# Down products of two feed-forward layers as seven block products, with weight sums made by DMA copies

## The chip, the cores and the metric

The kernel runs on one core of a Trainium2 chip. The metric is the device time of one execution in microseconds (us). The core has a matrix engine (TensorE, PE in the profile, with its weight loads as PEld), VectorE (DVE), ScalarE (ACT), GpSimd (POOL) and SyncE (SP), which run their own instruction queues and meet at semaphores. Sixteen DMA engines move data for transfers that SP, ACT and GpSimd issue.

## The reference

Three blocks work on one sequence of 1024 positions with 1024 features, all in float32. Each has a mixing part (gated linear attention and a short convolution; two kinds of attention and a long convolution; spatial gating and pooling) and a feed-forward part. The change touches the second product of the first and of the third feed-forward part:

```python
# first block
h = h + jnp.square(jax.nn.relu(hn @ w_up[layer])) @ w_down[layer]
out = rms_norm(h, norm_final_w)
# third block
f = jnp.square(jax.nn.relu(h @ w_fc1)) @ w_fc2
x = x + gate2 * rms_norm_3(f, norm2_post)
```

`w_up` is 1024x4096, `w_down` is 4096x1024; `w_fc1` and `w_fc2` have the same sizes. The second block has a gated feed-forward part of its own.

## The kernel before

Activations lie with features on the 128 partitions and positions along the free axis. Every large product is made of three matmuls (`mm3`, L428): an operand is split into a rounded part hi (ACT copies it, L319) and the rest lo (DVE subtracts, L305), and hi-hi, hi-lo and lo-hi are added in PSUM. A matmul has a 128x128 stationary tile and up to 512 moving columns.

The feed-forward parts are called f1, f2 and f3. Their up products (`up7`, L895) are already made of seven block products over the halves of features and positions. Its loop goes over groups g (16 in f1 and f3, 22 in f2), each with 84 matmuls. The results get a square of a relu (`relu2`, L907) and go to a DRAM scratch `gd` by DMAs of ACT's queue (L910); the products of half the features for the first groups are parked in `sd` and read back through GpSimd's queue (`start`, L957). DVE writes into slots that are parts of `X1`.

The down products (`down7`, L1029) go through `CHUNKS`: 2 or 4 contraction tiles at a time. For a chunk the values are loaded from `gd`, split into `Hh` and `Hl`, the weights are loaded and split into ring slots, and eight output tiles times two halves of positions follow, each with one PSUM bank, which DVE adds to `X` (ACT copies in the first chunk). In the last chunk the sums of squares for the next norm are made as well: `sq_add` (L525) squares on ACT and adds on GpSimd, or on DVE for the second sum that f1 and f2 need. For f1 and f2 the residual is added to `X` by four accumulating DMAs of GpSimd (L1066). f3 takes its last chunk in parts of 512, 256 and 256 columns (`quarters`), and its tail (`tail`, L2267) normalises, adds the residual and stores.

All weights and all values of a down product come through one `Stream` (L148). It knows the units in order; `load` (L178) issues a unit's DMA on SP into a raw buffer, `_split` (L203) splits it into a ring slot, and two units are loaded ahead. Ring A has four slots, ring B two more in a down stage. Up and down stages have four raw buffers, until `drop_raws` (L786) leaves two. "ada" units, weights of a conditioning vector, are spread over f1 and f2: DVE multiplies and adds them in eight instructions each (`ada_unit`, L634).

The order of work is written out by hand: the program keeps a count `pe` of matmul time and steps background generators (`fine`, `step`) and the stream (`tick`, L246) between groups of matmuls. Each engine takes its instructions in order.

Of the kernel before, what the change touches and what calls it, by code (L numbers as in the profile page):

```python
# [57 lines left out]

def _feat(a):

    return np.ascontiguousarray(a.T.reshape(KT, P, a.shape[0]).transpose(1, 0, 2))


def lay_out(i):
# [17 lines left out]
    a["w1_down"] = i["w_down"][0].reshape(32, P, D)  # L82
# [24 lines left out]
    a["w3_down"] = i["w_fc2_3"].reshape(32, P, D)  # L107
# [40 lines left out]
class Stream:  # L148
# [5 lines left out]
    def __init__(self, k):  # L154
# [6 lines left out]
        self.raws = []  # L161
        self.groom = [False, False]
# [40 lines left out]
    def _split(self):  # L203
# [62 lines left out]


class Kern:
    def __init__(self, tc, a, out):
# [7 lines left out]
        self.adap = None  # L277

# [373 lines left out]
    CHUNKS = {"f1": [2, 2] + [4] * 7, "f2": [2] + [4] * 5, "f3": [2, 2] + [4] * 7}  # L652
# [5 lines left out]
    def setup(self):  # L658
# [46 lines left out]
        def ffn7(n, up, down, with_ada=0):  # L705
# [19 lines left out]
            S[n + "h"], S[n + "d"] = [], []  # L725
            gd = S[n + "x"] = self.drp.tile([a[down].shape[0], P, T], F32, name="gd" + n)
# [168 lines left out]
    def up7(self, name):  # L895
# [11 lines left out]
        def relu2(dst, src, m, t, scale=1.0):  # L907
            self.act(dst, src, AF.Relu, scale=scale)
            self.act(dst, dst, AF.Square)
            nc.scalar.dma_start(out=gd[m, :, 512 * t:512 * t + 512], in_=dst)  # L910
# [12 lines left out]
        for g in range(0, M, 2):  # L923
# [7 lines left out]
            for i in (0, 1):  # L931
# [7 lines left out]
                else:  # L939
                    relu2(s, ps[i], 2 * (g + i), 0)  # L940
# [7 lines left out]
        def slot():  # L948
            n[0] += 1
            return X1[:, (n[0] - 1) % 8]  # L950
# [6 lines left out]
        def start(g):  # L957

            ca = wide() if gated else None
            s1 = None  # L960
            if g < M:
                s1 = scratch() if gated else slot()
                nc.gpsimd.dma_start(out=s1, in_=sd[g])
                if gated:
                    nc.gpsimd.dma_start(out=ca[:, :512], in_=cd[g])
            return s1, ca

        nxt = start(0)
        for g, G in enumerate(groups):
# [18 lines left out]
            if g >= M:  # L988
# [4 lines left out]
                else:  # L993
                    relu2(slot(), z, 2 * g, 0)
# [11 lines left out]
            if not gated:  # L1006
                relu2(c22, c22, 2 * g + 1, 1)
# [4 lines left out]
            else:  # L1012
                relu2(c21, c21, 2 * g + 1, 0)
# [9 lines left out]
            else:  # L1023
                relu2(v, v, 2 * g, 1)
        W.groom[1] = True
        self.ext_es.close()
        self.open_ss()

# [123 lines left out]
    def block1(self):  # L1152
# [9 lines left out]
        lvl = gp.tile([P, 7, P], U8, name="lvl")  # L1162
        g0, g0_es = self.pool("gate0", 1, None, "right")
# [177 lines left out]
        self.open_ring("f1d", ada=True)  # L1341
        g = self.cols("norm_final_w")
        self.tt(self.g12, g, self.cols("ln1_g_2"), ALU.mult)
        a1, a2 = [], []
        self.down7("f1", self.add_ffn(a1, a2, g),
# [167 lines left out]
    def block2(self):  # L1513
# [243 lines left out]

        self.up7("f2")
# [268 lines left out]
    def block3(self):  # L2027
# [204 lines left out]
        self.hp, e = self.pool("hp2", 1, None, "right")  # L2232
        self.ffn_es.insert(0, e)
        ac = []

        def add(m, part, ps, first, last):
# [88 lines left out]
```

## Time and profile before

| | us |
|---|---|
| three runs: median (lowest to highest) | 3528.7 (3525.08 to 3528.71) |
| profiled execution | 3526.44 |
| its span, first to last instruction | 3524.6 |
| PE busy in the span | 3419.4 |
| DVE busy | 2201.8 |
| ACT busy | 1367.4 |
| GpSimd busy | 335.8 |

The up stage of f1 ends near 806 us, its down stage near 1182; f2 runs from about 1890 to 2510; f3's up stage ends near 3143 and its down stage at 3509, with the last norm and the stores behind it. In rows of windows the columns are the stretch, its length, busy time of PE, PEld, DVE, ACT and POOL with the number of instructions in brackets, the granted PE clock as a share of 2.4 GHz, the share of the 16 DMA engines, and GB/s. In rows of groups they are line, engine, operation, out<-in, shapes, count, busy us and mean ns, then the idle time before them with what ended it. In rows of a timeline: start, duration, engine, line, operation, and in brackets the idle time before with its releaser.

### The profile page before, as it was taken

The numbers are of one execution on the slowest core, as the hardware profiler recorded it, in microseconds if no ns is written. First come the engines' busy times: TensorE is split into PE (matmuls) and PEld (weight loads), VectorE is DVE, ScalarE is ACT, GpSimd is POOL, SyncE is SP. The second block draws the span as 40 slices with busy tenths as digits, with TensorE's granted clock in tenths as the row PEclk, the third lists the DMA queues.
The fourth block names the chain that finished last, engine by engine and source line by source line (L and its number), as shares of the span: only waits on it lengthen the run. The fifth ranks groups of instructions, "written<-read, shape, count | busy, mean of one in ns | idle before, by whom it ended". The sixth has DMA issues, their size and how long they took to land. (4 is left out here: it accounts for less than half of the span.)

```text
span 3524.6 us, 43683 instructions
## 1 busy us (share of the span) xinstructions
PE 3419.4 (97%) x16725; PEld 2808.1 (80%) x16725; DVE 2201.8 (62%) x3747; ACT 1367.4 (39%) x2046; POOL 335.8 (10%) x368
## 2 busy tenths in 40 slices
PE   7999999999999989999999999999999999999998
PEld 7788898887888777876698788878778878877887
DVE  5456366556666574667768988867665676645444
ACT  3432244444112443555634444431332564451111
POOL 0111020000000210000020000000232410000003
PEclk9999999999999999998999999999999999999999
DMA  3111444336633186444325322274222154343222
GB/s 106 48 43 47 148 135 148 117 118 191 184 133 113 58 196 173 123 129 147 110 94 166 116 84 84 96 221 149 88 67 90 62 184 149 132 167 114 96 84 72
DMA packets 180964, 421.46 MB, mean 120 GB/s; under 512 B 18088, under 2 KB 58744, under 8 KB 180628
## 3 DMA queue, kind: packets, MB, share of 16 engines
q1 hardware_dynamic: 133044, 325.34, 28.8%
q10 hardware_dynamic: 38304, 67.13, 5.1%
q0 software_dynamic: 9408, 26.22, 3.6%
q8 instruction: 131, 2.15, 0.3%
q14 instruction: 77, 0.63, 0.1%
HBM read 304.50 MB, written 105.63 MB: 116 GB/s over the span
## 5 line engine op out<-in xcount | busy, mean ns | idle before, releaser
L324 PE MATMUL mm<-Hh,whi 128*128 128x512 f32 (+3 forms) x3632 | 1384.2, 381 | 11.7 <-DVE X L305 4.5
L324 PE MATMUL mm<-Hh,wlo 128*128 128x512 f32 (+3 forms) x3632 | 1365.6, 377 | 4.7 <-DVE wlo L305 4.7
L324 PE MATMUL mm<-Hl,whi 128*128 128x512 f32 (+3 forms) x3632 | 1369.6, 377 | 0.2 <-DVE Hl L305 0.2
L324 PEld LDWEIGHTS mm<-Hh,whi 128*128 128x128 f32 x3632 | 686.0, 189 | 155.3 <-issue 6.8
L324 PEld LDWEIGHTS mm<-Hh,wlo 128*128 128x128 f32 x3632 | 685.7, 189 | 138.5 <-DVE wlo L305 9.0
L324 PEld LDWEIGHTS mm<-Hl,whi 128*128 128x128 f32 x3632 | 686.1, 189 | 127.7 <-issue 1.4
L319 ACT ACTIVATE whi<-raw 128x1024 fp32r<-128x1024 f32 (+3 forms) x386 | 379.0, 992 | 694.6 <-PE mm L324 459.9
L305 DVE TENSOR_TENSOR wlo<-raw,whi 128x1024 fp32r<-128x1024 f32 (+3 forms) x386 | 441.7, 1151 | 193.3 <-ACT whi L319 182.8
L305 DVE TENSOR_TENSOR X<-X,mm 128x512 f32<-128x512 f32 (+1 forms) x446 | 290.3, 655 | 366.7 <-PE mm L324 362.1
L324 PE MATMUL mm<-t,whi 128*128 128x512 f32 x1296 | 408.6, 396 | 2.4 <-ACT whi L319 2.4
L324 PEld LDWEIGHTS mm<-t,whi 128*128 128x128 f32 x1296 | 242.9, 188 | 62.4 <-ACT whi L319 3.3
L324 PE MATMUL mm<-t,wlo 128*128 128x512 f32 x648 | 256.7, 396 | 1.9 <-DVE wlo L305 1.7
L319 ACT ACTIVATE Hh<-raw 128x1024 fp32r<-128x1024 f32 x86 | 89.6, 1057 | 364.8 <-PE mm L324 213.3
L321 ACT ACTIVATE X<-X 128x512 f32<-128x512 f32 (+1 forms) x226 | 151.9, 673 | 186.2 <-DVE X L310 153.7
L305 POOL TENSOR_TENSOR acc<-acc,sq 128x256 f32<-128x256 f32 (+1 forms) x108 | 115.9, 1074 | 910.0 <-ACT sq L321 906.4
L305 DVE TENSOR_TENSOR raw<-raw 128x512 f32<-128x512 f32 x216 | 145.2, 687 | 79.5 <-DMA raw<-in_w_up 77.1
L324 PEld LDWEIGHTS mm<-t,wlo 128*128 128x128 f32 x648 | 121.8, 188 | 33.4 <-DVE wlo L305 4.1
L305 DVE TENSOR_TENSOR Hl<-raw,Hh 128x1024 fp32r<-128x1024 f32 x86 | 104.6, 1222 | 56.9 <-ACT Hh L319 56.3
L310 DVE SCALAR_TENSOR_TENSOR ada<-raw,silc,ada 128x128 f32<-128x128 f32 x336 | 115.5, 350 | 8.3
L324 PE MATMUL mm<-whi,Hh 128*128 128x264 f32 (+4 forms) x336 | 111.7, 342 | 6.5 <-ACT Hh L319 2.8
L324 PE MATMUL mm<-wlo,Hh 128*128 128x264 f32 (+4 forms) x336 | 111.2, 340 | 2.4 <-DVE wlo L305 2.4
L310 DVE SCALAR_TENSOR_TENSOR X<-mm,X 128x512 f32<-128x512 f32 x108 | 74.5, 690 | 61.6 <-PE mm L324 60.1
(290 smaller groups left out, 3400.0 us busy)
## 6 DMA issues: line engine op xcount, KB each, us to landing
raw<-in_w_up SPq DMA_DIRECT2D x136, 512.0 KB
raw<-gdf SPq DMA_DIRECT2D x86, 512.0 KB
raw<-in_w_down SPq DMA_DIRECT2D x86, 512.0 KB
gdf<-X ACTq DMA_DIRECT2D x108, 256.0 KB
raw<-in_w_ada SPq DMA_DIRECT2D x48, 512.0 KB
gdf<-X ACTq DMA_DIRECT2D x22, 512.0 KB
B<-qd SPq DMA_DIRECT2D x36, 256.0 KB
A<-qd SPq DMA_DIRECT2D x36, 256.0 KB
```

Source lines behind the costliest of these rows:

```text
L305: eng.tensor_tensor(out=out, in0=a, in1=b, op=op)
L310: self.nc.vector.scalar_tensor_tensor(out=out, in0=a, scalar=s, in1=b, op0=op0, op1=op1)
L319: self.nc.scalar.activation(out, in_, f, scale=scale, **kw)
L321: self.nc.scalar.activation(out, in_, f, bias=bias, scale=scale, **kw)
L324: self.nc.tensor.matmul(out, l, r, start=s, stop=e, skip_group_check=grp)
```

## The change

The weights are laid out by quarters on the host (`_quarters`): a contraction tile's parity and a half of the outputs choose the quarter. `up7` no longer stores the two halves of its values; it stores seven pieces per group, of which three are the values themselves (pieces 0, 1 and 2) and four are made by four more DVE instructions, and writes these four through GpSimd's queue. Its slots are both halves of `X`. A new `sums` queues, for four of the seven products, DRAM-to-DRAM copies of a quarter on ACT's queue, kept in program order, and accumulating DMAs of another quarter, or of an earlier sum, on GpSimd's; `sums_step` is called from `tick` and issues one each 20 (f1, from the first block on) or 24 us (f3, from f2's up stage on) of counted matmul time. `down_parts` takes the place of `down7` for f1 and f3: seven products in the order P1, P2, P6, P7, P4, P5, P3, each of eight steps with one unit of weights and one of values, four output tiles in four PSUM banks; P2, P7 and P3 go on accumulating in the banks of the product before. Both operands come through the ring, and four units are loaded ahead until the last product. `X` (f1) or `Hh` (f3) is loaded with the residual by plain DMAs of GpSimd. f3's tail has one part of 512 columns per half, and f1 and f3 no longer use `CHUNKS`.

```diff
+def _quarters(w):
+    w = w.reshape(4, 2, 2, 2, P, 2, 512).transpose(0, 3, 5, 1, 4, 2, 6)
+    return np.ascontiguousarray(w).reshape(4, 4, 2, P, 2, 512)
...
-        while self.nd < min(self.ns + 2, len(self.seq)):
+        while self.nd < min(self.ns + self.ahead, len(self.seq)):
             self.load()
...
     def tick(self):
         self.k.ada_flush()
+        self.k.sums_step()
...
+    def sums(self, name, w, pace, at):
+        S = self.S[name + "s"]
+        late = []
+        for i, q, p in ((0, 1, 3), (1, 0, None), (2, 1, 0), (3, 2, None)):
+            for e in range(4):
+                r = slice(2 * e, 2 * e + 2)
+                self.sums_todo.append((self.nc.scalar, S[i, r], w[e, q], {}))
+                self.sums_todo += late
+                src = w[e, p] if p is not None else S[0 if i == 1 else 1, r]
+                late = [(self.nc.gpsimd, S[i, r], src, dict(accum_op=ALU.add, max_dma_last_dim=4096))]
+        self.sums_todo += late
+        self.sums_at = max(self.pe, at)
+        self.sums_pace = pace
+
+    def sums_step(self):
+        if self.sums_todo and self.pe >= self.sums_at:
+            eng, dst, src, kw = self.sums_todo.pop(0)
+            ins = eng.dma_start(out=dst, in_=src, **kw)
+            if not kw:
+                self.tc.keep_in_program_order(ins)
+            self.sums_at = self.pe + self.sums_pace
...
+                A = {i: [a[down][e // 2, q, e % 2] for e in range(8)]
+                     for i, q in (("P1", 0), ("P2", 2), ("P4", 3))}
+                A.update({"P5": sw[0], "P6": sw[1], "P7": sw[2], "P3": sw[3]})
+                for i in self.ORDER:
+                    for e in range(8):
+                        S[n + "d"].append([W.add(x[e].rearrange("p a b -> p (a b)"), D, n + "d")
+                                           for x in (A[i], gd[PIECE[i]])])
+                        if e % 2:
+                            ada(with_ada)
...
             else:
-                relu2(v, v, 2 * g, 1)
+                relu2(v, v)
+                t1_, t2_, t4_ = slot(), slot(), slot()
+                self.tt(t1_, ca, v, ALU.subtract)
+                self.tt(v, c22, v, ALU.subtract)
+                self.stt(t2_, t1_, -1.0, c22, ALU.mult, ALU.subtract)
+                self.stt(t4_, t2_, -1.0, c21, ALU.mult, ALU.subtract)
+                for i, t in ((3, t1_), (5, v), (4, t2_), (6, t4_)):
+                    nc.gpsimd.dma_start(out=piece(i, g), in_=t)
...
+    def down_parts(self, name, out, tail):
+        sp, e = self.pool("sums", 1, None, "right")
...
+        W.ahead = 4
+        new = True
+        for n, i in enumerate(self.ORDER):
+            if n == 6:
+                self.drop_raws()
+                W.ahead = 2
+            if new:
+                ps = [self.ps() for _ in range(4)]
+            for e in range(8):
+                wa, wb = (W.get(u) for u in D_[8 * n + e])
+                for m in range(4):
+                    for k in (0, 1):
+                        w, x = slice(k * 512 + m * P, k * 512 + m * P + P), slice(k * 512, k * 512 + 512)
+                        self.mm3(ps[m], wa.hi[:, w], wa.lo[:, w], wb.hi[:, x], wb.lo[:, x],
+                                 new and e == 0 and k == 0, e == 7 and k == 1, not new)
...
+                    if e == 7:
+                        z = ps[m]
+                        if i == "P1":
+                            self.act(s[:, m], z, AF.Copy)
+                        elif i == "P2":
+                            out(0, m, z, 1)
+                        elif i == "P6":
+                            self.tt(v[:, m], z, s[:, m], ALU.add)
+                        elif i == "P7":
+                            self.tt(s[:, m], z, s[:, m], ALU.add)
+                        elif i == "P4":
+                            out(0, 4 + m, z, -1, s[:, m])
+                        elif i == "P5":
+                            out(1, 4 + m, z, -1, s[:, m])
+                        else:
+                            out(1, m, z, 1, v[:, m])
+                    W.tick()
...
+            new = i not in ("P1", "P6", "P5")
+            if i == "P4":
+                self.unsummed = True
+                self.norms[0] = self.bg(tail((0, 0, 512)))
+            elif i == "P3":
+                self.unsummed = True
+                self.norms[1] = self.bg(tail((1, 512, 1024)))
...
+        self.sums("f1", a["w1_down"], 20.0, 60.0)
...
+        def out(half, m, z, sign, extra=None):
+            x = self.X[half][:, m]
+            op = ALU.add if sign > 0 else ALU.subtract
+            if extra is not None:
+                self.tt(x, x, extra, op)
+            self.tt(x, x, z, op)
...
+            self.sq_add(a1[half], x, got[half])
+            self.sq_add(a2[half], x, got[half], 0, g[:, m:m + 1], self.nc.vector)
+            got[half] += 1
...
+        self.sums("f3", a["w3_down"], 24.0, 0.0)
         self.up7("f2")
```

## Rows read from the trace of the kernel before

**Rows 1.** The page, parts 1 and 2: PE's busy time, the granted clock.
```profile
PE 3419.4 (97%) x16725; PEld 2808.1 (80%) x16725; DVE 2201.8 (62%) x3747; ACT 1367.4 (39%) x2046; POOL 335.8 (10%) x368
...
PEclk9999999999999999998999999999999999999999
```

**Rows 2.** Windows: f1 down, f2 up, f3 up, start of f3 down.
```profile
804.00:1152.00 348.00, 346.22 (x1521) 279.96 (x1519) 232.29 (x445) 85.18 (x100) 14.74 (x11) 1.00 0.50 155
1915.00:2310.00 395.00, 388.59 (x1663) 310.68 (x1662) 335.19 (x393) 175.46 (x191) 4.85 (x9) 1.00 0.30 104
...
2870.00:3137.00 267.00, 265.80 (x1142) 214.16 (x1141) 158.72 (x205) 128.87 (x182) 6.56 (x12) 1.00 0.43 143
3137.00:3182.00 45.00, 41.73 (x175) 31.98 (x174) 25.46 (x27) 28.24 (x39) 0.00 (x0) 1.00 0.72 244
```

**Rows 3.** Windows: a stretch in the middle of f3's down stage.
```profile
3330.00:3420.00 90.00, 90.00 (x388) 72.60 (x388) 40.36 (x49) 17.32 (x17) 0.00 (x0) 1.00 0.29 96
```

**Rows 4.** Groups of instructions from 804 to 1186 us, f1's down stage.
```profile
L305 DVE TENSOR_TENSOR X<-X,mm 128x512 f32<-128x512 f32 x129 | 87.6, 683 | 67.4 <-PE mm L324 66.9
L310 DVE SCALAR_TENSOR_TENSOR ada<-raw,silc,ada 128x128 f32<-128x128 f32 x196 | 67.9, 350 | 5.2
L305 DVE TENSOR_TENSOR wlo<-raw,whi 128x1024 fp32r<-128x1024 f32 x36 | 43.9, 1235 | 19.2 <-ACT whi L319 19.1
L319 ACT ACTIVATE whi<-raw 128x1024 fp32r<-128x1024 f32 x36 | 36.8, 1055 | 113.7 <-DMA raw<-in_w_down 65.5 <-PE mm L324 46.9 <-DMA raw<-in_w_g 0.9
```

**Rows 5.** Timeline of DVE in the first half of f1's last chunk.
```profile
1131.05 0.69 DVE L305 TENSOR_TENSOR X<-X,mm 128x512 f32<-128x512 f32 x1 [1.40 <-PE mm L324]
...
1134.04 1.79 DVE L305 TENSOR_TENSOR acc<-acc,sq 128x512 f32<-128x512 f32 x1
1135.76 0.67 DVE L305 TENSOR_TENSOR X<-X,mm 128x512 f32<-128x512 f32 x1
...
1137.74 1.52 DVE L305 TENSOR_TENSOR acc<-acc,sq 128x512 f32<-128x512 f32 x1 [0.18 <-ACT sq L321]
1139.18 0.67 DVE L305 TENSOR_TENSOR X<-X,mm 128x512 f32<-128x512 f32 x1
```

**Rows 6.** Timeline of ACT beside it.
```profile
1136.46 0.63 ACT L321 ACTIVATE sq<-X 128x512 f32<-128x512 f32 x1 [1.52 <-DVE X L305]
1137.00 0.71 ACT L321 ACTIVATE sq<-X,smalls 128x512 f32<-128x512 f32 x1
```

**Rows 7.** The chain that ended last (start, us), at f3's down.
```profile
3143.14 12.03 DMA raw<-in_w_down
...
3165.72 3.50 DMA raw<-in_w_down
...
3173.02 4.99 DMA raw<-in_w_down
```

**Rows 8.** Groups of instructions from 490 to 800 us, f1's up stage.
```profile
L310 DVE SCALAR_TENSOR_TENSOR X<-mm,X 128x512 f32<-128x512 f32 x30 | 20.7, 692 | 21.1 <-PE mm L324 20.6
...
L963 POOL DMA_DIRECT2D X<-sdf x8 | 4.5, 559 | 87.0 <-DVE raw L305 35.3 <-DMA gdf<-X 26.8 <-issue 15.2
```

**Rows 9.** Timeline of DVE in the last norm of f3.
```profile
3517.29 0.47 DVE L310 SCALAR_TENSOR_TENSOR X<-X,gp,ax 128x256 f32<-128x256 f32 x1
3517.68 0.41 DVE L305 TENSOR_TENSOR X<-X,xr 128x256 f32<-128x256 f32 x1
```

**Rows 10.** DMA issues: tile, queue, count, KB each, median us to landing.
```profile
X<-xd POOLq DMA_DIRECT2D x8, 1024.0 KB, 13.7
```

**Rows 11.** Windows: f1's down stage, with and without accumulating DMAs.
```profile
860.00:920.00 60.00, 60.00 (x267) 48.79 (x266) 39.30 (x83) 11.19 (x11) 5.18 (x4) 1.00 0.87 228
920.00:980.00 60.00, 60.00 (x267) 48.73 (x266) 41.60 (x86) 9.25 (x10) 0.00 (x0) 1.00 0.43 144
```

**Rows 12.** Windows: after the sums of f1's second half.
```profile
1194.00:1200.00 6.00, 6.00 (x16) 4.80 (x17) 2.77 (x18) 1.70 (x3) 0.00 (x0) 0.52 0.00 0
1200.00:1203.00 3.00, 3.00 (x15) 2.42 (x14) 0.00 (x0) 0.39 (x1) 0.00 (x0) 1.00 0.00 0
```

More of the change, by code (lines that the diff above doesn't have):

```diff
@@ L161, in __init__ @@
         self.raws = []
+        self.ahead = 2
         self.groom = [False, False]
@@ L277, in __init__ @@
         self.adap = None
+        self.sums_todo = []
+        self.sums_at = 0.0
     def col(self, name, j=0):
@@ L957, in start @@
         def start(g):
-            ca = wide() if gated else None
+            ca = wide() if gated else slot()
             s1 = None
@@ L1341, in block1 @@
         self.open_ring("f1d", ada=True)
+        for half in (0, 1):
+            for k in (0, 4):
+                nc.gpsimd.dma_start(out=self.X[half][:, k:k + 4],
+                                    in_=self.xd[:, k:k + 4, half * 512:half * 512 + 512])
         g = self.cols("norm_final_w")
@@ L1344, in block1 @@
         a1, a2 = [], []
-        self.down7("f1", self.add_ffn(a1, a2, g),
+        got = [0, 0]
+        def out(half, m, z, sign, extra=None):
[4 more added lines that the diff above has]
+            self.tt(x, x, z, op)
+            while half and self.unsummed:
+                self.fine(False, list(self.bgs))
+            if not got[half]:
+                a1.append(self.acc())
+                a2.append(self.acc())
+            self.sq_add(a1[half], x, got[half])
+            self.sq_add(a2[half], x, got[half], 0, g[:, m:m + 1], self.nc.vector)
+            got[half] += 1
+        self.down_parts("f1", out,
                  lambda part: self.norm2_gen(part, a1[part[0]], a2[part[0]], self.g12, None, g))
@@ L2231, in block3, with out @@
         self.open_ring("f3d")
[L2232 to L2233 removed]
+        xr = self.Hh.bitcast(F32)
+        for k in (0, 4):
+            nc.gpsimd.dma_start(out=xr[:, k:k + 4, :T], in_=self.xd[:, k:k + 4])
         ac = []
[L2236 to L2265 removed]
+        got = [0, 0]
+        def out(half, m, z, sign, extra=None):
+            x = self.X[half][:, m]
+            if extra is None:
+                self.act(x, z, AF.Copy)
+            elif sign > 0:
+                self.tt(x, z, extra, ALU.add)
+            else:
+                self.stt(x, z, -1.0, extra, ALU.mult, ALU.subtract)
+            if not got[half]:
+                ac.append(self.acc())
+            self.sq_add(ac[half], x, got[half])
+            got[half] += 1
         def tail(part):
@@ L2270, in tail @@
             self.unsummed = False
-            if half and len(xr) < 2:
-                t = self.hp.tile([P, KT, 512], F32, tag="h0", name="xr")
-                self.dma(t, self.xd[:, :, 512:])
-                xr.append([t[:, k] for k in range(KT)])
             yield self.after(1.0)
@@ L2287, in tail @@
                     f = self.X[half][:, k - 1, o:o + n]
-                    x = xr[half][k - 1]
-                    self.tt(f, f, x[:, o:o + n], ALU.add, gp if not half or k % 2 else None)
+                    self.tt(f, f, xr[:, k - 1, c0:c1], ALU.add, gp if not half or k % 2 else None)
                     self.dma(self.out[:, k - 1, c0:c1], f)
@@ L2292, in tail @@
             self.free(pb)
-        self.down7("f3", add, tail, quarters=True)
+        self.down_parts("f3", out, tail)
     def run(self):
```

71 lines of the change are left out of this document (35 added, 36 removed).

## The prediction, made before the change was run

> **What bounds the kernel now.** I read the page's first two parts first: TensorE is busy 97% of the span, at full clock in every slice but one [rows 1]. A busy PE need not be a useful one, so I then asked the windows for the stages that the change touches: in the down stage of f1 PE is busy 346.2 of 348.0 us, in the up stage of f3 265.8 of 267.0, and only the 45 us in which f3 goes from up to down hold 3.3 us of idle PE [rows 2]. Nothing else is near its end there: in the f1 down stage VectorE (DVE) has 232 of 348 us, ScalarE (ACT) 85, and the DMA engines half of theirs. So these stages last as long as their matmuls, and a matmul less is time less, until another engine's work comes to the front. In the middle of the f3 down stage 388 matmuls fill 90.00 us, 0.232 us each [rows 3].
>
> The sum is made against the profiled execution: 3526.4 us, of which 3524.6 are the span. The median of the runs is 3528.7, lowest 3525.1, so the profile stands in the middle of them.
>
> **What the change removes.** A down product is now 32 contraction tiles x 8 output tiles x 2 halves x 3 (hi-hi, hi-lo, lo-hi) = 1536 matmuls of 512 columns. Seven block products are 7 x 16 tiles x 4 output tiles x 3 = 1344. That is 192 less in f1 and in f3 each, 384 x 0.232 = **89.1 us less on PE**, all of it on the path, since PE has no idle time there to absorb it.
>
> **What it adds, term by term.**
>
> *Splits.* 32 + 32 operands are split into hi and lo now; then 7 x 16 = 112 are, 48 more per down. One costs ACT 1.06 and DVE 1.24 us [rows 4]: 51 and 60 us per down, off PE's path as long as both keep ahead. Against this DVE loses evacuations: about 128 adds of 0.68 us [rows 4] become 36. One step of a product (24 matmuls, 5.57 us) takes two units, so a unit is due each 2.78 us, and six ring slots are three steps, 11 us of lead. Cost: nothing while the lead lasts.
>
> *Borders between products in f1.* This is a new place. Four PSUM banks hold a product's four output tiles; the next product needs bank m again only three tiles (3 x 1.39 = 4.17 us) after it was finished. In f1 each finished tile also passes ACT twice for two sums of squares, and DVE adds the second. The timeline shows DVE keeping source order: accumulator reads due each 12 matmuls (2.78 us) after 1131.05 ran at 1135.76 and 1139.18, behind acc adds of 1.79 and 1.52 us [rows 5], which wait for ACT's 0.63 and 0.71 us [rows 6]. One tile, from its read to the end of its acc add, took 3.5 us, with a split hidden in the wait. At a border the tiles come each 1.39 us instead. For P4, whose tiles take one SBUF add more (0.69): a cycle of 4.2 us; the PSUM reads of tiles 2 and 3 end 10.1 and 14.3 us after tile 0 is done, and are due at 6.95 and 8.34: PE waits 6.0 us. For P5 the first tile has no acc add: last read at 11.5, 3.2 us late. For P2 (one add): 1.1. P1, P6 and P7 have one op per tile and wait for nothing. Sum **10 us**; bounds 0 (if ACT and DVE overlap better than in those rows) and 24 (a split of 1.2 us and part of an ada unit, eight ops of 0.35 [rows 4], between the reads of each border). In f3 a tile needs one DVE or ACT op and its sum is on GpSimd, so no border costs there.
>
> *The last product of f1* has two raw buffers (drop_raws) for 16 units and 4 ada units in 44.6 us. A buffer's round is landing (3.50 to 4.99 us in the quiet part of the chain [rows 7]), 2.3 of split and some 0.7 of issue, 6.5 to 8 us; two buffers give a unit each 3.2 to 4 us where 2.2 are wanted. Of the 20, some 10 are split or loaded when the product starts. **3 us**, bounds 0 and 8; in f3 there is no ada and I take 0.
>
> *The end of f1.* The last four tiles come in one burst; by the cycle above the last one's square is there 11 us after the last matmul. The first unit of the next stage covers part of it. **4 us**, bounds 0 and 8.
>
> *The two starts.* P1 takes two units a step from its first step; the first chunk before lasted 22 us for four. Now 3.3 us are lost in f3 and at most 1.8 in f1 [rows 2]; I take 3 each, so **2 us** more; bounds -4 and 8. The 12.03 us wait in the chain there [rows 7] is a load held up on SP's queue behind a load of a value written just before; P1 takes its values from the first piece in order, so that wait should go.
>
> *The up stages.* Four more DVE ops of 0.69 us per group [rows 8], 16 groups: 44 us in each of f1 and f3. In f3 DVE goes from 159 to 203 of 267 us (76%). The nearest row is the f2 up stage, with DVE at 335 of 395 us (85%), where PE is idle for 6.4 us [rows 2]. Six DMAs a group on GpSimd at 0.56 us of issue [rows 8] lie on an idle engine. **5 us** for both, bounds 0 and 12.
>
> *The end of f3.* Before, the last normalisation had 256 columns; now 512. Twelve ops on DVE of 0.47 and 0.41 us [rows 9] become about 0.69 each: 8.3 instead of 5.4 us, and the last burst and the larger last store add a little: **4 us**, bounds 3 and 6.
>
> *The copies and accumulations* (16 + 16 of 1 MB per weight). Each issue is a third of a microsecond on ACT or about 1.3 on GpSimd; a 1 MB accumulation lands 13.7 us after its issue [rows 10] and has 40 us. GpSimd waits in order for the copy, which was queued a pace of 20 or 24 us earlier behind ACT's work, and what queues behind it is the start of later norms, memsets and gate differences. The trace has no DRAM-to-DRAM copy; the nearest rows are two neighbouring stretches of f1's down stage: with the residual accumulations the DMA share is 0.87, without 0.43, and PE is busy 60.00 of 60 in both [rows 11]. **3 us**, bounds 0 and 12. f1's list ends by 700 us of the kernel's own count (some 760 real), its first reader comes after P1 and P2, near 890; it isn't late.
>
> Sum: -89.1 + 10 + 3 + 4 + 2 + 5 + 4 + 3 = -58. **3526.4 - 58 = 3468 us.**
>
> The Trainium skill ("DMA: Bandwidth & Descriptors", Issuing engines are not separate DMA queues) says that DMAs issued by SP, ACT and GpSimd end up on the same 16 engines and interleave, so the copies would take transfer time from the weight loads whoever issues them. The trace agrees on the sharing (0.87 against 0.43); by the rows it cost PE nothing at the old pace of loads, and by the rule it would show first in rival 3.
>
> **The rivals.**
>
> 1. *Nothing of this shows on PE*: DVE and ACT use the ring's lead at the borders. Only the 4 us of the last norm remain: 3526.4 - 89.1 + 4 = 3441. For it: f1's down stage has run without a stall; against: the order seen on DVE.
>
> 2. *DVE becomes the bound of f1's down stage.* 112 splits at 1.24 plus the 0.53 us that each waits for ACT (19.1 us over 36 [rows 4]) are 198; ada 28 x 2.8 = 78; 36 reads 24; 12 acc adds with their waits 12 x 2.8 = 34; half 0's norm some 8: 342 us for 312 of PE. f1 then loses 30 and the end, not 17: 3485, and to 3505 where reads and splits get in each other's way at borders too. For it: the f2 up stage's 85%; against: part of the waits overlaps.
>
> 3. *The loads don't keep up, and the kernel is slower.* Place: SP's loads into four raw buffers in both down stages. A down then reads 112 + 28 x 0.5 MB in about 320 us, near 240 GB/s where it was 155 [rows 2]. PE waits as soon as a unit takes over 2.78 us, and the whole gain is gone at 356 / 112 = 3.18 us a unit, which is a round of 12.7 us per buffer: a landing near 9.7. At the longest wait in the chain, 12.03 [rows 7], a round is 15, a unit 3.75, a down 420 us: 3526 + 2 x 64 = 3654. Just past the point it is 3530 to 3560. For it: the share of 0.72 at 244 GB/s [rows 2]; against: landings of 3.5 to 5 in the same stretch.
>
> 4. *The waits at the borders cool PE's clock.* After the sums of f1's second half the granted clock is 0.52 for 6 us, and 1.00 in the next stretch [rows 12], so a stretch like that ran at the 1.2 GHz level and cost near 2.8 us; PE had one-column matmuls and short waits just before. If the P4 and P5 borders and f1's end each bring one: 3468 + 3 x 2.8 = 3476. The Trainium skill ("TensorE: Matmul & The Clock Gate", HAM oscillation) has the same effect after idle gaps and would make each long border cost a slow stretch; no border of this kind is in this trace to decide it.
>
> 5. *The change doesn't do what it says*: copies that land late would hold up P6's loads. The slack of 130 us over 32 steps makes that need accumulations of some 25 us or more, twice the row. Its price is that excess times 16.
>
> **How the numbers follow.** The sum as it stands (3455 to 3485): 0.42. Rival 1 (3437 to 3455): 0.19. Rival 4: 0.10. Rival 2: 0.16. Rival 3: 0.09, of which 0.02 lands on no change. Rival 5: 0.04, half of it on no change. The range takes in all but the ends: rival 1 from 3439 up, rival 2 up to 3505. A measurement of this kernel can tell about 0.2%, 7 us, from no change: faster 0.87, same 0.04, slower 0.09.
>
> **What would show it.** The page should count 384 fewer 128x512 matmuls of the Hh kind (they appear under whi and wlo pairs), and PE idle should be read at the ends of P2, P4 and P5 in f1, with a read of PSUM on DVE as what ended it: 1, 6 and 3 us. In f3's down stage there should be none but at the start. DVE's share in f1's down stage should be 80 to 90%. If PE waits for wlo all along a product, rival 2 or 3 is right: with DVE busy it is 2, with ACT waiting for raw it is 3. I am wrong if PE stalls in the first or third block outside these stages, which would be the copies, or if the reads at borders overlap.

## The result, and the profile after

| | us | against the kernel before |
|---|---|---|
| kernel before, beside it | 3527.7 | |
| changed kernel, median | 3668.6 | 1.0396 [1.0384, 1.0409] |
| its profiled execution | 3663.3 | span 3661.5 |

The change makes the kernel 4% slower; 3468 was forecast. The page of the changed kernel, against [rows 1]: PE is busy for a smaller share of a longer span, and its granted clock is lower in three slices of the first block, where nothing but the sums' transfers was added, and in one of the third.

```profile
PE 3405.9 (93%) x16245; PEld 2767.8 (76%) x16245; DVE 2255.3 (62%) x3745; ACT 1442.0 (39%) x2113; POOL 447.8 (12%) x540
...
PEclk9999888999999999998999999999979999999998
```

Windows of the changed kernel, in the order f1 down, f2 up, f3 up, start of f3 down and a stretch in its middle; they answer to [rows 2, 3]:

```profile
895.00:1260.00 365.00, 336.71 (x1452) 266.71 (x1451) 248.60 (x436) 141.95 (x159) 26.63 (x24) 0.97 0.65 222
1983.00:2396.00 413.00, 391.12 (x1642) 312.33 (x1643) 329.13 (x375) 162.70 (x172) 14.14 (x21) 0.97 0.42 128
3059.00:3321.00 262.00, 251.88 (x1066) 198.35 (x1065) 178.71 (x251) 112.39 (x162) 42.94 (x79) 1.00 0.54 186
3321.00:3366.00 45.00, 45.00 (x195) 36.38 (x195) 24.48 (x24) 21.93 (x25) 2.96 (x5) 1.00 0.86 318
3470.00:3560.00 90.00, 90.00 (x401) 73.23 (x400) 44.68 (x46) 34.18 (x37) 4.02 (x3) 1.00 0.57 186
```

f3's down stage is as good as it can be: PE busy all 45 us of its start, where the kernel before lost 3.3, and all 90 us of the middle at a DMA share of 0.57. The loss is elsewhere. Three marks of the program cut it into four parts: the first matmul of each up stage that multiplies the tile `t`, read from TensorE's timeline. "No sums" and the four kernels after it are experiments, told below.

| lengths, us | to f1's up | to f2's up | to f3's up | to the last matmul |
|---|---|---|---|---|
| before | 532.7 | 1358.8 | 1000.2 | 622.7 |
| changed | 599.2 | 1383.7 | 1076.0 | 587.6 |
| no sums | 532.8 | 1341.6 | 994.0 | 589.5 |
| copies only | 568.7 | 1353.6 | 1042.2 | 590.7 |
| order without sums, transfers added | 533.1 | 1362.0 | 1013.8 | 587.0 |
| order with sums, transfers left out | 592.7 | 1370.2 | 1058.1 | 589.4 |
| free copies | 663.8 | 1336.6 | 996.8 | 590.6 |

The changed kernel lost 66 us in the first part, the mixing of the first block, in which f1's list of sums starts (it runs on to 882 us, in f1's up stage), 25 in the second part, 76 in the third, in which f3's list runs (from 1928 to 2869 us), and won 35 in the fourth, which has no sums.

### The profile page after: what moved, and what is told of

Its sections match the earlier page's. It is cut to its first block, busy times and chain, and to the rows that moved or that the text cites. A ratio compares the mean times of both kernels' runs of the same rounds, so it can differ in the third digit from the quotient of the medians.

```text
span 3661.5 us, 43367 instructions
## 1 busy us (share of the span) xinstructions
PE 3405.9 (93%) x16245; PEld 2767.8 (76%) x16245; DVE 2255.3 (62%) x3745; ACT 1442.0 (39%) x2113; POOL 447.8 (12%) x540
## 3 DMA queue, kind: packets, MB, share of 16 engines
q0 software_dynamic: 29984, 102.78, 11.5%
## 4 chain that ended last, share of the span: by engine, by line
PE 58%; DVE 13%; DMA 10%; issue 3%; ACT 3%; POOL 1%; SPq 0%; DVEq 0%; ACTq 0%; POOLq 0%
PE mm L337 50%; PE ax L337 5%; DVE wlo L318 4%; DMA raw<-in_w_ada 3%; DMA raw<-in_w_up 2%; PE o L337 2%; DVE X L318 2%; DMA raw<-gdf 2%; DVE X L323 2%; DVE ada L323 1%; DMA cb<-cs 1%; DVE raw L318 1%; ACT whi L332 1%; DMA raw<-in_w_down 1%; DVE Hl L318 0%
## 5 line engine op out<-in xcount | busy, mean ns | idle before, releaser
L337 PE MATMUL mm<-Hh,whi 128*128 128x512 f32 (+3 forms) x2576 | 979.3, 381 | 39.9 <-DVE X L318 14.5
L337 PE MATMUL mm<-Hh,wlo 128*128 128x512 f32 (+3 forms) x2576 | 967.0, 377 | 23.8 <-DVE wlo L318 23.6
L337 PE MATMUL mm<-Hl,whi 128*128 128x512 f32 (+3 forms) x2576 | 968.7, 376 | 2.6 <-DVE Hl L318 2.5
L318 DVE TENSOR_TENSOR wlo<-raw,whi 128x1024 fp32r<-128x1024 f32 (+3 forms) x546 | 645.4, 1195 | 390.0 <-ACT whi L332 383.9
L337 PEld LDWEIGHTS mm<-Hh,whi 128*128 128x128 f32 x2576 | 492.7, 191 | 147.0 <-DVE X L318 21.6
L337 PEld LDWEIGHTS mm<-Hh,wlo 128*128 128x128 f32 x2576 | 491.6, 191 | 122.1 <-DVE wlo L318 35.7
L337 PEld LDWEIGHTS mm<-Hl,whi 128*128 128x128 f32 x2576 | 492.3, 191 | 89.4 <-DVE Hl L318 4.2
L337 PE MATMUL mm<-whi 128*128 128x512 f32 x896 | 358.8, 401 | 7.8 <-ACT whi L332 2.9
L337 PE MATMUL mm<-wlo,whi 128*128 128x512 f32 x896 | 355.0, 396 | 2.5 <-DVE wlo L318 2.5
L337 PE MATMUL mm<-whi,wlo 128*128 128x512 f32 x896 | 355.3, 397 | 0.0
```

Source lines behind the costliest of these rows:

```text
L318: eng.tensor_tensor(out=out, in0=a, in1=b, op=op)
L337: self.nc.tensor.matmul(out, l, r, start=s, stop=e, skip_group_check=grp)
```

## The experiments

### Is it the sums at all?

The list of sums is left empty:

```diff
-        if self.sums_todo and self.pe >= self.sums_at:
+        if False:
-                A.update({"P5": sw[0], "P6": sw[1], "P7": sw[2], "P3": sw[3]})
+                A.update({i: [a[down][e // 2, q, e % 2] for e in range(8)]
+                          for i, q in (("P5", 1), ("P6", 0), ("P7", 1), ("P3", 2))})
```

> Leaves out the weight sums: no copies, no accumulations; the products that want a sum of quarters read a plain quarter instead, by loads of the same size. Theory A (the copies and accumulations cost nearly all that was lost, directly and through the order of the work around them): block 1, o1, f1 up, f2 up, f2 down and block 3 give back 66 + 11 + 25 + 17 + 34 us and the gain of f3's down stage (44 us) and of f1's (10 us and more) stays, with some 14 us lost in each of the two up stages: 3490 to 3515 us. Rival B (the pieces, the residual loads, the ring with four units ahead cost it): block 1 recovers at most, 3600 us or more.

Measured: 3476.7 us, 0.9858 [0.9841, 0.9876] of before. Rival B falls and theory A holds, though the time is 13 us under its range: the products, pieces, splits and borders make the kernel 51 us faster, and the 64 transfers of the sums turn that into 141 us slower. They cost 192 us, where the prediction had 3.

### Is it GpSimd waiting?

In the changed kernel the longest new wait of GpSimd (POOL) is on accumulations whose copy hasn't landed. POOL's waits over the whole span (line, releaser, total us, times, longest):

```profile
POOL swf L685 <- DMA swf<-in_w_down: 429.0, 17, 62.3
```

Three kernels change what it waits for: the accumulations pinned too, the accumulations left out, the copies no longer pinned.

```diff
             ins = eng.dma_start(out=dst, in_=src, **kw)
-            if not kw:
-                self.tc.keep_in_program_order(ins)
+            self.tc.keep_in_program_order(ins)   # e2_in_order
+            # e3_copies_only: as before the edit, but nothing is issued where kw is set
+            # e4_free: neither line
```

> The accumulations on GpSimd are kept in program order too; nothing is left out. Theory A1 (GpSimd's queue reaches an accumulation too early and stands until ACT's copy has landed, and what queues behind it comes late): GpSimd waits of 429 us for copies fall below 100, and 3500 to 3540 us. Rival A2 (the copies themselves, by transfer time or by their place on ACT's queue, are the price): within 20 us of the changed kernel, 3645 to 3690 us.

> Leaves out the accumulations; the 32 copies on ACT stay as they are, and the products read the copied quarter. Theory A1 (GpSimd's waits are the price): as without any sums, 3490 to 3530 us. Rival A2 (the copies on ACT's queue in program order are the price): 3600 us and more.

> The copies are no longer kept in program order, so they stand on ACT's queue wherever their operands allow, early; nothing is left out. Theory A1 (accumulations wait for copies that ACT reaches late): the copies have landed long before, GpSimd waits little, 3500 to 3540 us. Rival A2 (transfers of the copies and accumulations against the loads): all 32 MB move in fewer and denser stretches, at least the 3668 us of the changed kernel.

Measured: 3714.3 (1.0536 [1.0518, 1.0555]), 3565.8 (1.0110 [1.0095, 1.0125]) and 3604.4 (1.0222 [1.0205, 1.0239]). The same view of the first of them:

```profile
POOL swf L685 <- DMA swf<-in_w_down: 177.9, 5, 51.3
```

None of the three times lies in a range of either theory. The wait fell by 250 us, though not below the 100 that A1 asked, and the kernel became 46 us slower. Theory A1 falls: GpSimd's wait is real but not the price. Copies alone, for which nobody waits on GpSimd, cost 89 us, which is less than A2 said, and A2 didn't say how. In the kernel with free copies the last of both lists is issued at 612 us: its first part took 131 us more than without sums, and the rest ran within 6 us of it (table above). So the loss lies in the parts in which the transfers stand, whatever waits for them.

The windows of the instructions on the tile `pa` alone (a chain of small products in the first block; columns as in [rows 2], engines that have none left out) show what else is different there. Without sums:

```profile
190.00:240.00 50.00, 6.97 (x96) 5.82 (x96) 8.89 (x14) 1.00 0.10 32
240.00:290.00 50.00, 6.97 (x96) 5.82 (x96) 8.14 (x12) 1.00 0.14 43
340.00:390.00 50.00, 3.69 (x52) 2.93 (x50) 5.42 (x8) 1.00 0.17 53
390.00:460.00 70.00, 0.00 (x0) 0.00 (x0) 0.00 (x0) 1.00 0.54 188
```

The changed kernel:

```profile
190.00:240.00 50.00, 2.32 (x32) 1.94 (x32) 2.31 (x4) 1.00 0.12 43
240.00:290.00 50.00, 8.72 (x96) 7.72 (x96) 9.00 (x14) 0.94 0.48 127
340.00:390.00 50.00, 5.26 (x64) 4.39 (x64) 3.87 (x6) 0.97 0.34 95
390.00:460.00 70.00, 9.28 (x96) 8.01 (x96) 9.31 (x14) 0.85 0.48 158
```

Without sums the chain advances evenly, 96 small products per 50 us between dense ones, and is over by 390 us. In the changed kernel it falls behind by two thirds of a stretch at 190 us, and 96 of its products are left for 390 to 460; from 417 to 439 us these and other small products run with no dense one between them. Of the 66 us lost in this part some 30 are idle time of PE (32.0 us from 90 to 599 us, 2.5 without sums) and the rest is a lower clock: 0.94 from 90 to 460 us and 0.73 from 530 to 599, where it is 1.00 without sums. TensorE's order is different, though no matmul was added there. That gave a new theory, O: the order that the build gives the program is another once it has the transfers to place, and this order is the price.

### Order or transfers?

A first pair, with the kernel before as a control, was to hold the order fixed by building in source order:

```diff
-    with tile.TileContext(nc) as tc:
+    with tile.TileContext(nc, linearize=True) as tc:
```

> Leaves out the weight sums as before, and every engine takes its instructions in the order of the source; the build no longer rearranges them. It is the base for the next kernel, which has the same order on every engine but for the 64 transfers of the sums. The source order is near the one built without sums (on TensorE 1 row in 8 of the kernel before stands elsewhere): 3470 to 3560 us by both theories.

> The whole change, in the order of the source, nothing left out. Theory O (the price of the sums is the order: the build plans with the megabyte transfers and moves the rest of the work around them): with the order held, the 64 transfers cost at most 20 us over the kernel without sums in source order. Rival T (their transfer time, and GpSimd standing at an accumulation until its copy has landed): 80 us or more over it, as 3668 is 192 over 3476.

> The kernel before in the order of its source, as a control for the two others: what the order alone costs or brings without the change. Both theories: within 60 us of 3528.

Measured: 13870, 14328 and 13239 us. The expected times missed by far, and though 458 us over the kernel without sums lies in rival T's range, the pair says nothing on the order: this way of building also serialises the engines (in the first kernel the busy times of PE, DVE, ACT and POOL add up to 9859 us and cover 9810). What it gives is the price of a transfer when nothing runs beside it: (14328 - 13870) / 64 = 7.1 us. The next pair pins each engine's own order by edges that carry no wait:

```diff
+        for ins in nc.cur_bb.bb.instructions:      # before the build orders them
+            e = ins.engine
+            if e in last and ...:                  # one of PE, ACT, DVE, POOL, SP
+                tc.add_manual_dep(ins, last[e].name, mybir.DependencyInfo(
+                    mybir.DependencyClass.NoSync, mybir.DependencyReason.DATA), reason="order")
+            last[e] = ins
```

> Leaves out the weight sums as before. Every engine has its instructions pinned in the order of the source, with no waits but those of the data. (The pair before this one also had each instruction wait for the one before it on the other engines: it measured 457 us for 64 transfers one by one, 7.1 us each, and nothing on the order.) Base of the next kernel; the order is near that of the kernel without sums: 3460 to 3560 us by both theories.

> The whole change, nothing left out, each engine pinned in the order of the source: TensorE and VectorE have the same order, row by row, as in the kernel beside it without sums; only the 64 transfers are added. Theory O (the build's plan, which counts the megabyte transfers, moves the other work, and this is the price): at most 30 us over the kernel without sums, 3470 to 3570 us. Rival T (the transfers and the waits for them are the price whatever the order): 100 us or more over it.

Measured: 4100.5 (1.1624 [1.1605, 1.1644]) and 4113.2 (1.1645 [1.1623, 1.1668]). With the order held the sums cost 13 us, little more than the spread of the runs, as theory O has it; but in the source order the kernel takes 4100 us where the build's order takes 3477 and at most 3560 was expected, and a kernel with so much idle time may hide transfers. So I took a good order: the program is built once without the sums, and the order that each engine got is pinned, by the same kind of edge, on the real program; a copy or an accumulation stands behind the instruction that precedes it in the source. The mirror pins the changed kernel's order on a program without the transfers.

```diff
+    order = order_without_sums(new, arrays)     # q1; r1: the order of the changed kernel
     with tile.TileContext(nc) as tc:
-        body(tc, a, out)
+        sums = body(tc, a, out)                 # r1: the list of sums left empty
+        pin(tc, nc, order, sums)
```

> The whole change, nothing left out. The build is first made without the 64 transfers of the sums, and the order that it gives each engine (that of the kernel of 3477 us without sums) is then pinned on the real program; each copy and each accumulation stands behind the instruction of its engine that precedes it in the source. Theory O (the build plans with the transfers and moves the other work, and that order is the price): 3475 to 3510 us, faster than the kernel before. Rival T (the transfers and the waits for them): 3600 us or more.

> The mirror of it: the order that the build gives with the sums, which is that of the changed kernel, pinned on a program in which the 64 transfers are left out; the products read plain quarters. Theory O: the order alone costs nearly all, 3600 to 3670 us. Rival T: without transfers and waits nothing is lost, 3470 to 3500 us. If both have a share, it falls between, and the two kernels give each share.

| us | no transfers | 64 transfers | transfers cost |
|---|---|---|---|
| order built without sums | 3476.7 | 3513.9 | 37 |
| order built with sums | 3628.4 | 3668.6 | 40 |
| order costs | 152 | 155 | |

The ratios are 0.9858 [0.9841, 0.9876], 0.9964 [0.9952, 0.9975], 1.0295 [1.0278, 1.0312] and 1.0396 [1.0384, 1.0409]. The two prices add: the order cost 152 to 155 us, four fifths, and the transfers 37 to 40. That the edits held the order is seen in the traces: TensorE's 16245 instructions have the same sequence of operations and tiles in the two kernels of a row of the table, and of one row's sequence only 13271 can be matched, in order, with the other's. Theory O's range for the first kernel (3475 to 3510) was missed by 4 us, and its range for the mirror holds. All engines in two stretches of the first block, the order with sums but no transfers first:

```profile
240.00:290.00 50.00, 45.44 (x299) 41.35 (x297) 22.43 (x38) 12.66 (x18) 8.00 (x10) 0.95 0.14 43
...
390.00:460.00 70.00, 65.75 (x374) 54.27 (x373) 36.62 (x72) 18.59 (x29) 9.53 (x10) 0.87 0.45 147
```

and the order without sums, with the transfers:

```profile
240.00:290.00 50.00, 49.18 (x376) 44.04 (x375) 30.58 (x63) 15.63 (x24) 8.97 (x14) 1.00 0.32 93
...
390.00:460.00 70.00, 70.00 (x373) 59.74 (x373) 27.15 (x48) 18.82 (x33) 11.60 (x11) 1.00 0.65 218
```

The stall and the lower clock come with the order and without a single transfer (65.75 of 70 us, 0.87); with the transfers, in the order without sums, PE is busy 70.00 of 70 at full clock. In this kernel GpSimd still waits 169.2 us for copies: 27.7 of them in the first part, which is 0.3 us longer than without sums, and 110.4 in f2's up stage, which is 11 us longer.

### What are the 37 us?

> As the kernel with the plan made without the sums (3514 us), with the accumulations left out and the copies where they were; the products read the copied quarters. Theory Q (GpSimd's stand at accumulations is most of the 37 us): 3477 to 3488 us. Rival (the transfers' own time, in which a copy of 1 MB lands in 5 to 8 us and an accumulation in 8 to 15): the copies keep a third or more, 3490 to 3505 us.

> As the kernel with the plan made without the sums (3514 us), each accumulation replaced by a plain transfer of the same megabyte, from the same queue and at the same place, with the same wait for the copy before it; so the sums are left out, the transfers are not. Theory W (the price of about 34 us is where an accumulation stands on GpSimd's queue and what stands behind it): 3505 to 3515 us. Rival R (it is what an accumulation moves: it reads its target as well, and lands in 8 to 15 us where a plain copy takes 5 to 8): 3480 to 3495 us.

```diff
+            if kw:                        # q3_copies, with the pace kept
+                return
+            kw.pop("accum_op", None)      # q7_plain
```

Measured: 3480.1 (0.9862 [0.9844, 0.9880]) and 3491.6 (0.9901 [0.9885, 0.9917]). In the held order the copies cost 3 us, which is within the spread of the runs, where with the build's own order they cost 89: again the order. A plain megabyte in the place of each accumulation costs 11 us more, and that it accumulates another 22. The time lies in R's range, but neither alone is the whole: a third is the place and the transfer, two thirds that the transfer accumulates. DMA issues of the order without sums (tile, queue, count, KB each, median us to landing), first as it is, then with plain transfers:

```profile
swf<-in_w_down POOLq DMA_DIRECT2D x16, 1024.0 KB, 11.4
swf<-swf POOLq DMA_DIRECT2D x16, 1024.0 KB, 9.1
```

```profile
swf<-in_w_down POOLq DMA_DIRECT2D x16, 1024.0 KB, 6.6
swf<-swf POOLq DMA_DIRECT2D x16, 1024.0 KB, 5.8
```

One place where it reaches PE is seen in f1's up stage of the kernel with the order without sums, in the timelines of POOL, DVE and PE:

```profile
598.80 0.97 POOL L688 DMA_DIRECT2D swf<-in_w_down  x1
599.39 0.96 POOL L1023 DMA_DIRECT2D X<-sdf  x1
...
611.52 2.02 DVE L318 TENSOR_TENSOR raw<-raw 128x512 f32<-128x512 f32 x3 [7.30 <-DMA raw<-in_w_up]
...
617.21 0.79 PE L337 MATMUL mm<-Hh,whi 128*128 128x512 f32 x1 [6.69 <-DVE X L318]
```

An accumulation is issued at 598.80. A weight load of half the size, issued 2.1 us later by SP, lands after 10.6 us; the same load without sums lands after 4.9. DVE stands 7.30 us for it (1.60 without sums) and PE 6.69 (1.00). The stall costs more than its length: in the 4 us behind it the granted clock is 0.50, the lower level, and 9 matmuls run where a full clock has 17. The Trainium skill ("DMA: Bandwidth & Descriptors", Issuing engines are not separate DMA queues), which the prediction weighed, has it so: the load came from another engine and was held up all the same. From the first to the last matmul on `t`, f1's up stage takes 288.9 us here and 278.1 without sums, f2's 398.6 and 388.0; the rest of the 37 us, some 17, falls outside the up stages and was not followed up.

### Is there a better place for them?

Four kernels keep the order without sums and move the lists; four further copies stand between a copy and its accumulation, three more than before.

```diff
-        self.sums("f1", a["w1_down"], 20.0, 60.0)
+        self.sums("f1", a["w1_down"], 12.0, 20.0)     # q2, q4, q6; q5: both lists here, 6.5, 10.0
-        self.sums("f3", a["w3_down"], 24.0, 0.0)      # q6 leaves it
+        self.sums("f3", a["w3_down"], 12.0, 0.0)      # q2: ahead of the attention loop
         self.up7("f2")
+        self.sums("f3", a["w3_down"], 13.0, 0.0)      # q4
```

> As the kernel with the plan made without the sums (3514 us), but both lists stand elsewhere: f1's runs at 12 us of counted time from the start of the first block and is done before f1's up stage, f3's runs at 12 us through the attention of the second block and is done before f2's up stage; an accumulation follows its copy by three further copies. Nothing is left out. Theory Q (the 37 us left are GpSimd standing at accumulations in the up stages, where loads of X queue behind them, and loads that land later there): 3477 to 3492 us. Rival (transfer time costs the same wherever it falls): 3505 to 3525 us.

> As the kernel with both lists early (3530 us), but f3's list runs at 13 us of counted time from the start of f2's down stage through the third block's mixing part; f1's stays in the first block. Nothing is left out. By milestones f1's list in the first block cost some 7 us up to 1180, the attention lost 30 with f3's list in it, and in the kernel of 3514 the list cost 18 us in f2's up stage and none after it. Theory Q (the price is where GpSimd's queue or a short load is on the path: attention and the up stages): 3480 to 3495 us. Rival (transfers cost the same wherever they fall, about 0.5 us each): 3505 to 3520 us.

> As the kernel before it, but both lists in the first block and o1, all 64 transfers at 6.5 us of counted time. Nothing is left out. Theory Q: the first block has its loads' slack and GpSimd's work there is not on the path in the held order, so 64 cost little more than 32 did: 3480 to 3500 us. Rival (a list costs by its transfers): 3505 us or more.

> Nothing is left out. f1's list in the first block as in the kernel of 3516 us (it cost 5 us there up to f1's up stage and 10 up to f2), f3's list as in the kernel of 3514 us, from f2's up stage on at 24 us of counted time (20 us), accumulations three copies behind. If the two places add: 3477 + 10 + 20 = 3507, 3500 to 3512 us. Rival: the accumulations three copies behind pile up before f2's down stage as they did in the kernel of 3516 us, and it is no better than 3514.

Measured: 3529.7 (0.9999 [0.9989, 1.0008]), 3515.8 (0.9967 [0.9957, 0.9978]), 3523.2 (0.9994 [0.9984, 1.0005]) and 3512.4 (0.9956 [0.9939, 0.9972]). No place was free, so Q as put falls; q4's and q5's times are those of the rival, but a price that is the same everywhere it is not. Against the kernel without sums, f1's list at 12 us in the first block costs 3 to 5 us up to f1's up stage and 10 to 11 up to f2's (q4, q6), where at 20 us it costs 21 (q1). With f3's list in the attention (q2) the second part takes 34 us more, and with both lists in the first block (q5) the first part takes 23 and the second 36 more. f3's list cost 32 in f2's down stage and the third block (q4), where its waiting accumulations bunch behind f2's residual ones. POOL's timeline and the window of all engines there:

```profile
2361.14 1.29 POOL L1193 DMA_DIRECT2D X<-xd  x1 [4.05 <-ACT Hh L332]
2361.88 4.21 POOL L690 DMA_DIRECT2D swf<-in_w_down  x4
...
2340.00:2410.00 70.00, 54.63 (x218) 43.35 (x218) 35.97 (x78) 8.14 (x8) 6.23 (x6) 0.90 0.95 257
```

The four land 23 to 45 us after their issue, the DMA share is 0.95, and PE stands 15 of 70 us (3 in the same stretch without sums). In q6 they bunch again, and its third part takes 28 us more where 20 were expected. q6 has the lowest time of the kernels that leave nothing out, 0.4% below the kernel before and 4.3% below the change; q1, which only fixes the order, can't be told from it (0.9964 and 0.9956, with intervals that overlap).

## Why the prediction was wrong

**The step that failed is the term for the copies and accumulations**: 3 us, bounds 0 and 12; measured 192. It had two faults. The first is what it counted: the issues, what queues behind them on GpSimd, and the transfers, each beside work that was taken to stay in its place. But the diff adds the transfers to a program whose order is made by the build, only the copies are pinned, and the order of everything around them came out anew: 152 us. The prediction itself wrote that stalls in the first or third block would prove it wrong; it had the sign to look for and no price for it. The second is the bound on the transfers: the stretches of f1's down stage in which accumulating DMAs cost PE nothing [rows 11] have ample time for each load. In the up stages, which both lists reach, a load that lands 6 us later was a stall where it was looked at. The transfers cost 37, three times the upper bound.

**The rest of the sum**, read from the kernel without sums: it comes to 3526 - 61 = 3465, measured 3476.7, in the profiled execution 3472.3. The 7 us to the latter are for the most part misses that cancel: the up stages cost 18 us more than their term, while f3's down stage with its end came out some 7 us shorter, and the third part 6 (994.0 for 1000.2), for which the sum has no term.

- *Removed matmuls*: right. Windows of f3's down stage there, whole and middle:

```profile
3136.00:3451.00 315.00, 315.00 (x1369) 255.07 (x1368) 158.69 (x147) 123.88 (x135) 32.39 (x24) 1.00 0.59 200
3280.00:3370.00 90.00, 90.00 (x397) 73.13 (x396) 44.68 (x46) 34.63 (x37) 4.03 (x3) 1.00 0.57 187
```

The product's 1344 matmuls, and 25 small ones, take 315 us without a stall, 0.234 each where 0.232 was taken; the splits cost nothing, DVE is at 50%. The page has 480 instructions fewer, not 384: 288 of 512 columns and 192 of 256, since f3's last chunk was cut into parts before; in columns this is the same.

- *f1's borders, last product, end and start*: 18 us forecast. The window of that stage without sums:

```profile
813.50:1168.00 354.50, 339.38 (x1481) 269.77 (x1479) 254.61 (x447) 141.44 (x159) 28.78 (x24) 0.99 0.67 227
```

PE is idle 15.1 us (354.50 - 339.38), with 3.9 more at the end of f1 behind it. PE's waits in the window:

```profile
PE mm L337 <- DVE mod L318: 5.5, 3, 2.7
PE ax L337 <- DVE ada L323: 4.0, 5, 1.6
PE mm L337 <- ACT whi L332: 1.7, 3, 1.0
...
PE mm L337 <- DVE X L318: 1.1, 1, 1.1
PE mm L337 <- ACT s__6732 L332: 1.0, 1, 1.0
```

The size is right, in part by luck. The waits at the borders add up to 7.6 us where 10 were forecast, but not where they were forecast (`mod` is the DVE instruction behind the read of the bank that PE waits for): 2.7 behind P2 for 1.1, 1.1 behind P4 for 6.0, none behind P5 for 3.2, and 1.0, 0.7 and 2.1 behind P1, P6 and P7, which were to wait for nothing. So the cycle of reads and sums on DVE that gave 6.0 and 3.2 did not run as reckoned. In the changed kernel the idle time is 28.3 us. PE's longest wait there, in the changed kernel and then in the one with its order and no transfers:

```profile
PE ax L337 <- DVE ada L323: 19.6, 4, 9.8
```

```profile
PE ax L337 <- DVE ada L323: 17.5, 4, 8.3
```

So this wait too came with the order.
- *The up stages*: 5 us forecast, bounds 0 and 12; mis-sized. f1's and f3's up stages there, then PE's longest wait in f3's:

```profile
532.80:813.50 280.70, 275.52 (x1177) 220.13 (x1176) 189.03 (x260) 126.80 (x182) 38.76 (x71) 1.00 0.51 177
...
2868.40:3133.00 264.60, 253.13 (x1068) 198.78 (x1067) 178.84 (x251) 112.73 (x163) 43.16 (x79) 1.00 0.53 185
...
PE mm L337 <- DVE X L318: 10.5, 14, 1.1
```

The same two stages of the kernel before, from the first matmul on `t` to about the last:

```profile
532.70:803.30 270.60, 270.60 (x1164) 218.34 (x1163) 149.74 (x195) 123.56 (x176) 2.16 (x4) 1.00 0.38 125
...
2891.70:3140.00 248.30, 248.30 (x1068) 200.31 (x1067) 144.23 (x191) 113.32 (x161) 4.31 (x8) 1.00 0.40 135
```

f3's took 16 us more for the same 1068 matmuls. f1's took 10 more, of which 3 are 13 matmuls that fall into the stretch: 23 in all. The prediction took f2's 85% of DVE as its nearest row and read a share, while the price is an order: in f3's groups where PE waits, about nine of the 16, three of the four new instructions stand ahead of the one that it waits for. DVE's timeline in one group, and PE's:

```profile
2972.00 0.68 DVE L318 TENSOR_TENSOR X<-X,X 128x512 f32<-128x512 f32 x1
...
2973.74 0.68 DVE L318 TENSOR_TENSOR X<-X,X 128x512 f32<-128x512 f32 x1
2974.34 0.68 DVE L323 SCALAR_TENSOR_TENSOR X<-X 128x512 f32<-128x512 f32 x1
2974.94 0.68 DVE L318 TENSOR_TENSOR X<-mm,X 128x512 f32<-128x512 f32 x1
...
2975.68 0.50 PE L337 MATMUL mm<-Hh,whi 128*128 128x512 f32 x1 [0.95 <-DVE X L318]
```

The 14 waits are 0.75 us each. PE's idle time makes 11.5 of f3's 16 us; what the rest is was not found.

- *The two starts*: 2 us; PE has no idle time in f3's start now, as the prediction said of the 12.03 us wait.
- *The end of f3*: 4 us; from the last product to the end of the span 19.3 us, before 15.6 from 3509.

**The rivals.** None of them made the time. Against rival 1 there are the 15.1 us of idle PE. DVE is at 72% of f1's down stage (254.61 of 354.50), where the prediction had 80 to 90, so rival 2 is out. Rival 3 had the right resource and the wrong place: in the down stages the loads keep up at a share of 0.57 to 0.67, and the load seen to come late was behind an accumulation in an up stage. Rival 4 did happen in f1's down stage, where it was placed, but small: without sums the granted clock is 0.62 for 4 us behind P2's border and again behind P7's, and 11 and 12 matmuls run there where the next 4 us have 18 and 20, some 3 us in all; no border did it in f3 (1.00 throughout). The copies were not late for P6 (rival 5): f1's last accumulation is issued at 882 us, and the first load of a sum at 981. The chance of 0.09 for slower was on a mechanism that is not the one that ran; a case "the added transfers shift the order of other work" was missing.

**What stays open.** That the order changes with the transfers is shown by the two programs; why the build moves the chain on `pa` behind is not in any trace. The pin holds all engines at once, so which engine's order costs most is not known, and where the order costs the 64 us of the third part (1058.1 against 994.0) was not looked at. Nor was it settled why f3's list cost more in the attention (q2) than at a slower pace from f2's up stage on (q1, q6).

## What to carry to other kernels

Where a build orders the instructions, an added DMA can cost more by the new order than by its transfer, four times as much here: pin the order of the work around it, or build without it and take over that order, before anything is said of its price. A two-by-two of order and operation separates the two in two kernels. An accumulating transfer cost most here where a short load behind it was on the path, and where several stood behind one another on a queue that reached them late; no place that was tried was free.

## What was not expected of the hardware

An accumulation of 1 MB from DRAM to DRAM took 9.1 to 11.4 us to land and a plain transfer from the same queue and place 5.8 to 6.6; with 32 of the first the kernel took 22 us more. Beside one of them a weight load landed in 10.6 instead of 4.9 us. GpSimd stood 169 us on waits for copies in a kernel that lost 37 us in all. And where a chain of small products ran for 22 us with no dense product between them, the granted clock was 0.85 over the 70 us around it, so partly at the 1.2 GHz level, after short waits of PE; between dense products the same chain kept 1.00.
